# The second tile's residual sum, norm and transposes placed behind the first tile's product, at the start of a gated unit

## The chip, the cores and the metric

The kernel runs on one core of one Trainium2 chip, as one launch. The metric is device time in microseconds (us), from three timed runs of the kernel before. Beside them stands one execution that the hardware profiler recorded, and every row below comes from that one. Its engines are PE (TensorE, with PEld for its weight loads), DVE (VectorE), ACT (ScalarE), POOL (GpSimd) and SP (SyncE, whose queue issues nearly all loads).

## The reference, cut to what matters

Two blocks run one after the other over 256 tokens of width 1024. The first has two layers, and the change lies in it:

```
def swiglu(x, w_gu, w_down):
    gate, up = jnp.split(x @ w_gu, 2, axis=-1)
    return (jax.nn.silu(gate) * up) @ w_down

def hybrid_layer(x, mem_n, ...):
    h = layer_norm(DEEPNORM_ALPHA * x + 0.5 * swiglu(x, ffn1_w_gu, ffn1_w_down), ln_g[0], ln_b[0])
    ...                     # mixer: delta rule, window attention, memory attention, gates
    h = layer_norm(DEEPNORM_ALPHA * h + merged @ w_out, ln_g[1], ln_b[1])
    return layer_norm(DEEPNORM_ALPHA * h + 0.5 * swiglu(h, ffn2_w_gu, ffn2_w_down), ln_g[2], ln_b[2])
```

So each layer has two gated units (`swiglu`), and the second of them takes what the norm `ln_g[1]` gives. The second block (five mixers and a sparse expert layer that gathers table rows) is not touched.

## The kernel before, in words

**Tiles.** The 256 tokens are two tiles of 128, `x[0]` and `x[1]` (the rows name them x_74 and x_75). A gated unit multiplies with 22 column units of 1 MB each (256 columns: 128 of gate, 128 of up). A unit's weights arrive in a buffer `raw` (three of them) and are split by `unit` (line 203) into two parts of 1024 columns; of each part ACT writes a rounded copy `hi` (line 211, a CAST) and DVE, for some parts POOL, the rest `lo = raw - hi` (line 215). A product is three passes: hi by hi, hi by lo, lo by hi (`mm3`, line 232). The activations are split the same way: `transposed` (line 285) turns 128x128 pieces on PE, ACT copies four at a time to `xt0` (line 294), DVE subtracts to `xt1` (line 295).

**A gated unit (`ffn`, line 364).** The first two column units are multiplied token tile by token tile in `cols_first` (line 260; the rows call its product p_gx): 48 matmuls for the first tile, then 48 for the second. The first two units' split weights go to buffers named `hx` and, for the last `lo`, to the ring. The other 20 units (p_gu) take both tiles at once. Between them, at units 2 and 5, `mem_side` norms and transposes one tile of the memory input (`m`, with its gains `mgb`).

**The junction.** `add_norm` (line 421) loads the norm's gains and biases into `gb` (1 MB, each row of it broadcast to all partitions), and then per tile adds the residual (line 432, once per half of 512 columns), norms it (`norm`, line 297: statistics in line 304, eight one-column instructions of `rsqrt`, then lines 309 and 310 per half), and transposes it. In the kernel before it runs for both tiles in `first` (line 891) before the second gated unit of a layer begins (line 925), in the same space of buffers as the projection `out_proj`, whose last products it waits for. The gated unit at the very start has its own short form: `start(0)` loads and transposes the first tile, and `start(1)`, called by `early` behind the split of the first two units, does so for the second. Its first two units are loaded in halves of 512 KB.

**What sets the order.** The program is written through a layer with a scheduler, which fixes one order of instructions per engine when the program is built; each engine then runs its list in that order. Instructions written earlier in the program come first where the scheduler has a choice. SP's list is the order of the loads.

Of the kernel before, what the change touches and what calls it, by code (L numbers as in the profile page):

```python
# [21 lines left out]
L = 2  # L22
NT = T // P
# [4 lines left out]
ALPHA = (2 * L) ** 0.25  # L28
# [146 lines left out]
class _Kernel:  # L175
# [56 lines left out]
    def mm3(self, out, A, B, first, last):  # L232

        for n, (i, j) in enumerate(((0, 0), (0, 1), (1, 0))):
            self.nc.tensor.matmul(out, A[i], B[j], start=first and n == 0, stop=last and n == 2)  # L235
# [7 lines left out]
    def toks(self, outs, w, xt, k0, first, last):  # L243

        nk = len(w[0])
        for k in range(nk):
            for tt in range(NT):
                self.mm3(outs[tt], [t[:, tt, k0 + k] for t in xt], [t[k] for t in w],
                         first and k == 0, last and k == nk - 1)
# [7 lines left out]
                    self.mm3(outs[tt], [t[:, tt, k0] for t in xt], [t[k] for t in w], k0 == 0, k0 == n - 1)  # L257
                    k0 += 1

    def cols_first(self, name, ws, xt):  # L260

        out = []
        for tt in range(NT):
            p = self.bank([2, 2 * P], "mm", name)
            for i, w in enumerate(ws):
                for k in range(KT):
                    self.mm3(p[:, i], [t[:, tt, k] for t in xt], [t[k] for t in w], k == 0, k == KT - 1)
            out.append(p)
        return out
# [91 lines left out]
        self.nc.sync.dma_start(self.pc, self.a["pc"][l])  # L361


    def ffn(self, l, which, xt, side=(), early=None):


        nc = self.nc
        ht = [self.work.tile([P, NT, NF, P], F32R, tag=f"ht{i}", name=f"ht{i}", bufs=1) for i in range(2)]
        gu, dn = self.a["gu" + which], self.a["dn" + which]
        side = list(side)  # L370
        ws = [self.unit(gu[l, f], KT, 2 * P, LO if early else 0, None if early else self.in_work(6, ("hi", "lo")[:2 - f]), pieces=2 if early else 1)
              for f in range(2)]
        if early:
            early()
        for tt, p in enumerate(self.cols_first("p_gx", ws, xt)):
            s = self.work.tile([P, 2, P], F32, tag="silu", name="silu", bufs=2)
            h = self.work.tile([P, 2, P], F32, tag="hid", name="hid", bufs=2)
            nc.scalar.activation(s, p[:, :, :P], AF.Silu)
            nc.vector.tensor_mul(h, p[:, :, P:], s)
            self.transposed(h.rearrange("p a b -> p (a b)"), 2, ht, tt)  # L380
        for f in range(2, NF):
            w = self.unit(gu[l, f], KT, 2 * P)
            p = self.bank([2, T], "mm", "p_gu")
            for j in range(2):
                self.feat(p[:, j], w, xt, j * P)
            s = self.work.tile([P, T], F32, tag="silu", name="silu", bufs=2)
            h = self.work.tile([P, T], F32, tag="hid", name="hid", bufs=2)
            nc.scalar.activation(s, p[:, 0], AF.Silu)
            nc.vector.tensor_mul(h, p[:, 1], s)
            h = h.rearrange("p (t c) -> p t c", t=NT)  # L390
            nc.scalar.copy(ht[0][:, :, f], h)
            nc.vector.tensor_tensor(ht[1][:, :, f], h, ht[0][:, :, f].bitcast(F32), op=OP.subtract)
            if side and f % 3 == 2:
                side.pop(0)()
        y = [[self.bank([512], "acc", "p_y") for _ in range(2)] for _ in range(NT)]
        self.down(y, lambda b, **k: self.unit(dn[l, b], 2, D, **k), NF // 2, lambda b: ht, lambda b: 2 * b,
                  (self.in_work(6, ("hi",)), self.in_work(6)))
        return y
# [22 lines left out]
    def add_norm(self, l, i, x, y, coef, then=None):  # L421


        nc = self.nc
        gb = self.work.tile([P, 2, D], F32, tag="gb", name="gb", bufs=1)
        self.bcast(gb.rearrange("p a b -> p (a b)"), self.a["ln"][3 * l + i], 2 * D)
        xt = self.xt_tiles()
        for tt in range(NT):
            z = x[tt]
            for h in range(2):  # L430
                sl = slice(512 * h, 512 * h + 512)
                nc.vector.scalar_tensor_tensor(z[:, sl], y[tt][h], coef, z[:, sl], op0=OP.mult, op1=OP.add)
            self.norm(z, z, gb, LN_EPS / ALPHA ** 2)
            if then:
                then(z, xt, tt)
            else:
                self.transposed(z, KT, xt, tt)
        return xt

    def x_tile(self, tt):  # L440
        return self.state.tile([P, D], F32, tag=f"x{tt}", name=f"x{tt}", bufs=1)
# [449 lines left out]
    def first(self):  # L891
        nc, a, tc = self.nc, self.a, self.tc
        x = [self.x_tile(tt) for tt in range(NT)]
        xt = self.xt_tiles()
        self.memkv, self.memkv2 = {}, {}
        mems = [(a["mem"], "ln", a["ln"][3 * L])] * 2 + [(a["mem2"], "rms", a["nrm"][2 * L + l]) for l in range(L)]
        with tc.tile_pool(name="kv", bufs=1) as kv:
            for l in range(L):
                for k in range(2):
                    n = 2 * l + k  # L900
                    with self.space(f"f{n}"):
                        early = None
                        if n == 0:
                            def start(tt):
                                nc.sync.dma_start(x[tt], a["x"][:, tt])
                                self.transposed(x[tt], KT, xt, tt)

                            start(0)
                            early = lambda: (start(1), self.load_gain(0))
                        memT, side = self.mem_side(*mems[n])  # L910
                        y = self.ffn(l, str(k + 1), xt, side, early)
                        xt = self.add_norm(l, 2 * k, x, y, 0.5 / ALPHA, None if n < 2 * L - 1 else self.rms_xt)
                        if n < L:
                            self.memkv[n] = self.mem_kv(n, memT, kv)
                        else:
                            self.memkv2[n - L] = self.mem_kv2(n - L, memT)
                    if k == 0:
                        with self.space(f"m{l}"):
                            merged = self.work.tile([P, NT, D], F32, name="merged", bufs=1)
                            with self.space(f"mi{l}"):  # L920
                                self.load_small(l, ROW_AT["pool_scale"][0])
                                self.mixer(l, x, xt, merged)
                            with self.space(f"mo{l}"):
                                y = self.out_proj(l, merged)
                                xt = self.add_norm(l, 1, x, y, 0.5 / ALPHA)
        return x, xt


# [577 lines left out]
```

## Time and profile before

| | |
|---|---|
| median of 3 runs (lowest to highest) | 3100.79 us (3097.57 to 3101.62) |
| the profiled execution, its own time | 3095.72 us |
| its span, first to last instruction | 3093.9 us |
| mean granted TensorE clock | 0.979 |
| PE busy | 2770.6 us, 90% of the span |
| DVE busy | 2131.5 us, 69% |
| ACT busy | 1490.1 us, 48% |
| PE share of the chain that ended last | 48% |

Busy PE time comes from modelled ends of pipelined matmuls, so 90% is a share of time in which PE had something in flight. The first half of the span (the first block, to about 1420 us) is a chain of PE work, and the second half is mostly waiting for gathered table rows. The mean clock of 0.979 says that PE runs at the upper of its two levels (2.4 GHz) nearly always, and at the lower one (1.2 GHz) in short stretches.

The two junctions that the change moves lie at 500 to 530 us (layer 0) and 1215 to 1245 us (layer 1), and the program's start at 0 to 24 us.

### The profile page before, as it was taken

Reading aid. Unit: us, or ns where it says so; the run is one execution under the profiler, and the core shown is the slowest. Engines: PE = TensorE matmul, PEld = TensorE weight load, DVE = VectorE, ACT = ScalarE, POOL = GpSimd, SP = SyncE. Lnnn points to the kernel's source line nnn. Section 1 sums busy time; section 2 is a strip of 40 time slices with the busy share of each in tenths; the row PEclk is TensorE's granted clock in tenths of the full one; section 3 lists DMA queues with packets and bytes.
Section 4 is the critical chain, followed back from the end, with each engine's and each line's share of the span. In section 5 each row is a group of like instructions: output and inputs, shape, how many; then the busy total and the mean of one; then the engine's idle time right before and its main releaser. Section 6 shows DMA issues by size and latency. Waiting matters only on the chain.

```text
span 3093.9 us, 40461 instructions
## 1 busy us (share of the span) xinstructions
PE 2770.6 (90%) x13968; PEld 2000.1 (65%) x13968; DVE 2131.5 (69%) x4878; ACT 1490.1 (48%) x3196; POOL 814.4 (26%) x596
## 2 busy tenths in 40 slices
PE   9999999999999999999979887877789788978777
PEld 8988988989989887997855443322258544423222
DVE  6558667656558658657976776867578777777764
ACT  5446444444436444544645544544446454445444
POOL 0003220000003221000124444554411344445553
PEclk9999999999999999999989999999999899999999
DMA  7545325555554334556259999999962699999998
GB/s 262 182 171 176 116 89 205 197 194 194 183 184 171 116 109 149 205 186 220 82 195 425 426 421 423 427 427 427 427 229 75 264 426 426 422 426 427 426 427 347
DMA packets 121739, 841.82 MB, mean 272 GB/s; under 512 B 14016, under 2 KB 16832, under 8 KB 22208
## 3 DMA queue, kind: packets, MB, share of 16 engines
q0 software_dynamic: 73728, 536.90, 41.3%
q1 hardware_dynamic: 47520, 301.82, 27.4%
q8 instruction: 111, 1.82, 0.2%
q14 instruction: 92, 0.75, 0.1%
q10 hardware_dynamic: 288, 0.52, 0.0%
HBM read 838.15 MB, written 1.05 MB: 271 GB/s over the span
## 4 chain that ended last, share of the span: by engine, by line
PE 48%; DMA 22%; DVE 20%; issue 4%; ACT 3%; POOL 2%; POOLq 0%; DVEq 0%; SPq 0%; ACTq 0%
DMA uv<-in_puv_dram,idx 18%; PE p_gu L235 15%; PE p_y L235 11%; DVE uv L1391 5%; PE p_g L235 4%; DMA raw<-in_puv_dram,idx 4%; PE p_y L1399 2%; PE p_b L235 2%; POOL uv L1388 2%; PE p_gx L235 1%; DVE lo L215 1%; PE p_s L235 1%; DVE conv L542 1%; PE p_c L235 1%; PE p_tr L292 1%
## 5 line engine op out<-in xcount | busy, mean ns | idle before, releaser
L1399 PE MATMUL p_y<-uv,dgw 128*128 128x512 f32 x1788 | 868.6, 623 | 221.5 <-ACT dgw L1397 220.1
L1399 PEld LDWEIGHTS p_y<-uv,dgw 128*128 128x128 f32 x1788 | 324.8, 195 | 722.0 <-ACT dgw L1397 438.4
L1391 DVE SCALAR_TENSOR_TENSOR uv<-uv,xg 128x1024 f32<-128x1024 f32 x447 | 542.9, 1221 | 290.3 <-DMA uv<-in_puv_dram,idx 149.1
L211 ACT CAST hi<-raw 128x1024 fp32r<-128x1024 f32 (+1 forms) x488 | 502.3, 1034 | 472.8 <-PE p_gu L235 121.8
L215 DVE TENSOR_TENSOR lo<-raw,hi 128x1024 fp32r<-128x1024 f32 (+1 forms) x410 | 501.8, 1229 | 310.0 <-ACT hi L211 301.6
L1388 POOL DMA_INDIRECT uv<-in_puv_dram,idx x447 | 529.3, 1184 | 671.5 <-PE p_y L1399 248.4
L215 POOL TENSOR_TENSOR lo<-raw,hi 128x1024 fp32r<-128x1024 f32 (+1 forms) x78 | 197.3, 2530 | 1499.6 <-ACT hi L211 1276.8
L235 PE MATMUL p_gu<-xt,hi 128*128 128x256 f32 x2560 | 463.6, 284 | 0.0
L1394 ACT ACTIVATE wt<-act,rms_r 128x1 f32<-128x1 f32 x512 | 150.3, 294 | 569.2 <-DVE uv L1391 486.1
L235 PEld LDWEIGHTS p_gu<-xt,hi 128*128 128x128 f32 x2560 | 399.3, 192 | 0.0
L235 PE MATMUL p_gu<-xt,lo 128*128 128x256 f32 x1280 | 362.6, 283 | 0.0
L235 PEld LDWEIGHTS p_gu<-xt,lo 128*128 128x128 f32 x1280 | 245.6, 192 | 0.0
L1397 ACT ACTIVATE dgw<-ident,wt 128x128 f32<-128x128 f32 x512 | 205.0, 400 | 15.2
L235 PE MATMUL p_y<-hi,ht 128*128 128x512 f32 x576 | 181.3, 395 | 0.0
L235 PE MATMUL p_c<-xt,hi 128*128 128x256 f32 x960 | 179.8, 287 | 0.2
L1399 PE MATMUL p_y<-raw,dgw 128*128 128x512 f32 x260 | 129.8, 622 | 32.6 <-ACT dgw L1397 32.4
L1395 ACT ACTIVATE wt<-wt,gate 128x1 f32<-128x1 f32 x512 | 150.6, 294 | 16.0
L235 PEld LDWEIGHTS p_c<-xt,hi 128*128 128x128 f32 x960 | 150.6, 192 | 1.9 <-ACT sh L1095 0.7
L235 PE MATMUL p_c<-xt,lo 128*128 128x256 f32 x480 | 137.3, 287 | 0.0
L235 PE MATMUL p_y<-lo,ht 128*128 128x512 f32 x320 | 126.3, 395 | 0.0
L235 PE MATMUL p_g<-hi,xt 128*128 128x512 f32 x384 | 125.6, 400 | 0.0
L235 PEld LDWEIGHTS p_y<-hi,ht 128*128 128x128 f32 x576 | 108.5, 188 | 25.2
(524 smaller groups left out, 4275.2 us busy)
## 6 DMA issues: line engine op xcount, KB each, us to landing
raw<-in_gu_dram SPq DMA_DIRECT2D x86, 1024.0 KB, 4.8
raw<-in_dn_dram SPq DMA_DIRECT2D x44, 1024.0 KB, 4.8
raw<-in_win_t_dram SPq DMA_DIRECT2D x30, 1024.0 KB, 4.8
raw<-in_win_g_dram SPq DMA_DIRECT2D x24, 1024.0 KB, 4.8
raw<-in_wout_dram SPq DMA_DIRECT2D x18, 1024.0 KB, 4.9
raw<-in_wq_dram SPq DMA_DIRECT2D x16, 1024.0 KB, 9.4
raw<-in_wbr_dram SPq DMA_DIRECT2D x12, 1024.0 KB, 4.8
raw<-in_win_s_dram SPq DMA_DIRECT2D x8, 1024.0 KB, 6.9
```

The source lines that it names most:

```text
L211: self.nc.scalar.copy(hi, r)
L215: engine.tensor_tensor(lo[:, a:b], r[:, a:b], hi[:, a:b].bitcast(F32), op=OP.subtract)
L235: self.nc.tensor.matmul(out, A[i], B[j], start=first and n == 0, stop=last and n == 2)
L292: nc.tensor.transpose(p[:, j], x[:, (g + j) * P:(g + j + 1) * P], self.ident)
L542: nc.vector.scalar_tensor_tensor(c[:, s:], th[:, j, :T - s], pc[:, 4 * f + 3 - s:4 * f + 4 - s], c[:, s:], op0=OP.mult, op1=OP.add)
L1388: nc.gpsimd.indirect_dma_start(out=r, out_offset=None, in_=a["puv"], in_offset=bass.IndirectOffsetOnAxis(ap=idx[:, tt, h, k:k + 1], axis=0))
L1391: dot = nc.vector.scalar_tensor_tensor(r[:, :D], r[:, :D], 1.0, xg[tt], op0=OP.mult, op1=OP.mult, accum_out=act)
L1394: nc.scalar.activation(wt, act, AF.Gelu, scale=rs[tt])
L1395: nc.scalar.activation(wt, wt, AF.Copy, scale=gate[:, tt, h, k:k + 1])
L1397: nc.scalar.activation(dg, self.ident, AF.Copy, scale=wt)
L1399: nc.tensor.matmul(y[tt][half], dg, r[:, D + 512 * half:D + 512 * half + 512], start=n == 0, stop=n == HEADS * TOPK - 1)
```

## The change

`cols_first` gets a function `arrive` and calls it for each tile just before that tile's product. `add_norm` no longer runs its loop over tiles; it loads the gains and returns `arrive(tt)`, which does what the loop did for one tile. For the second gated unit of each layer this `arrive` is handed to `ffn`, where the first two units' weights are already split (in program order) when it is called for tile 0, and tile 0's product stands between it and tile 1. `add_norm` now also takes its buffers from the gated unit's space, where `gb` and `mem_side`'s `mgb` share one buffer. At the end of a gated unit both tiles are called at once, as before. At the start of the program the loads of `x[0]` and `x[1]` both stand behind the first two units.

```diff
-    def cols_first(self, name, ws, xt):
+    def cols_first(self, name, ws, xt, arrive):
...
         for tt in range(NT):
+            arrive(tt)
             p = self.bank([2, 2 * P], "mm", name)
...
-        if early:
-            early()
-        for tt, p in enumerate(self.cols_first("p_gx", ws, xt)):
+        for tt, p in enumerate(self.cols_first("p_gx", ws, xt, arrive)):
...
         xt = self.xt_tiles()
-        for tt in range(NT):
+
+        def arrive(tt):
             z = x[tt]
...
-        return xt
+
+        return xt, arrive
...
-                        early = None
                         if n == 0:
-                            def start(tt):
+                            def arrive(tt):
                                 nc.sync.dma_start(x[tt], a["x"][:, tt])
                                 self.transposed(x[tt], KT, xt, tt)
-
-                            start(0)
-                            early = lambda: (start(1), self.load_gain(0))
+                                if tt:
+                                    self.load_gain(0)
+                        elif k == 1:
+                            xt, arrive = self.add_norm(l, 1, x, y, 0.5 / ALPHA)
+                        else:
+                            arrive = lambda tt: None
                         memT, side = self.mem_side(*mems[n])
-                        y = self.ffn(l, str(k + 1), xt, side, early)
-                        xt = self.add_norm(l, 2 * k, x, y, 0.5 / ALPHA, None if n < 2 * L - 1 else self.rms_xt)
+                        y = self.ffn(l, str(k + 1), xt, side, arrive, n == 0)
+                        xt, arrive = self.add_norm(l, 2 * k, x, y, 0.5 / ALPHA, None if n < 2 * L - 1 else self.rms_xt)
+                        for tt in range(NT):
+                            arrive(tt)
...
                                 y = self.out_proj(l, merged)
-                                xt = self.add_norm(l, 1, x, y, 0.5 / ALPHA)
```

The scheduler's new order shows at three places. (Line numbers behind line 264 are one higher in the changed kernel up to `ffn`; line 309 of before is line 310 there, and 310 is 311.)

First, DVE at the junction of layer 0 in the kernel before, from the first tile's last gain (x_74) to the second tile's (x_75):

```order
L310 SCALAR_TENSOR_TENSOR x_74<-x_74,ln_r,gb 128x512 x2
L432 SCALAR_TENSOR_TENSOR x_75<-p_y,x_75 128x512
L304 BN_STATS ln_st<-x_75 128x6
L295 TENSOR_TENSOR xt_4921<-p_tr,xt_4920 128x512 x2
L305 BN_AGGR ln_mv<-ln_st 128x2
L276 TENSOR_SCALAR rs_w<-ln_mv 128x1
L309 SCALAR_TENSOR_TENSOR x_75<-x_75,ln_mv,gb 128x512 x2
```

The first tile is finished before the second tile's last residual sum (L432), and no weight split (L215) stands between them.

The same place on DVE in the changed kernel, from behind that residual sum and its statistics:

```order
L215 TENSOR_TENSOR hx<-raw,hx 128x1024
L306 BN_AGGR ln_mv<-ln_st 128x2
L215 TENSOR_TENSOR hx<-raw,hx 128x1024
L277 TENSOR_SCALAR rs_w<-ln_mv 128x1
L215 TENSOR_TENSOR lo<-raw,hx 128x1024
L278 TENSOR_SCALAR rs_y<-rs_w 128x1
L310 SCALAR_TENSOR_TENSOR x_74<-x_74,ln_mv,gb 128x512 x2
L310 SCALAR_TENSOR_TENSOR x_75<-x_75,ln_mv,gb 128x512 x2
L215 TENSOR_TENSOR lo<-raw,hx 128x1024
L215 TENSOR_TENSOR lo<-raw,hi 128x1024 x2
L279 TENSOR_TENSOR rs_h<-rs_y 128x1
L305 BN_STATS ln_st<-m 128x6 x2
```

The next row there is the first tile's last gain (L311 on x_74). Six weight splits, both tiles' L310 and the memory tile's statistics have moved ahead of it. In layer 1 the order is the same but for those statistics.

Second, PE at the same junction, before:

```order
L292 MATMUL p_tr<-ident,x_74 128x128 x8
L292 MATMUL p_tr<-ident,x_75 128x128 x8
L235 MATMUL p_gx<-hx,xt_4920 128x256 x3
L235 MATMUL p_gx<-hx,xt_4921 128x256
L235 MATMUL p_gx<-hx,xt_4920 128x256 x2
```

And in the changed kernel:

```order
L293 MATMUL p_tr<-ident,x_74 128x128 x8
L235 MATMUL p_gx<-hx,xt_4925 128x256 x2
L235 MATMUL p_gx<-hx,xt_4926 128x256
L235 MATMUL p_gx<-hx,xt_4925 128x256 x2
L235 MATMUL p_gx<-hx,xt_4926 128x256
```

The second tile's eight transposes (x_75) have left this place and stand, in two groups of four, inside the products.

Third, SP's loads at the program's start, before (x_74 is the first token tile) and changed:

```order
L355 DMA ident<-in_c_ident_dram 128x128
L905 DMA x_74<-in_x_dram 128x1024
L200 DMA raw<-in_gu_dram 128x1024 x4
L905 DMA x_75<-in_x_dram 128x1024
L331 DMA gain<-in_nrm_dram 128x1024
```

In the changed kernel the same five read:

```order
L356 DMA ident<-in_c_ident_dram 128x128
L200 DMA raw<-in_gu_dram 128x1024 x4
L905 DMA x_74<-in_x_dram 128x1024
L905 DMA x_75<-in_x_dram 128x1024
L332 DMA gain<-in_nrm_dram 128x1024
```

The first token tile's load has gone from the second place to the sixth of SP's loads. At the junctions `gb` is loaded behind three weight units where it stood behind one, and `mgb`, which now waits for the last reader of `gb`, behind six where it stood behind three.

## Rows read from the trace of the kernel before

**Rows 1.** Timeline of PE, layer 0: start, duration (us), instruction, count, idle before.
```profile
504.90 2.96 PE L235 MATMUL p_y<-hx,xt 128*128 128x512 f32 x12
507.90 1.29 PE L292 MATMUL p_tr<-ident,x 128*128 128x128 f32 x8
514.53 1.94 PE L292 MATMUL p_tr<-ident,x 128*128 128x128 f32 x8 [5.33 <-DVE x L310]
516.12 5.51 PE L235 MATMUL p_gx<-hx,xt 128*128 128x256 f32 x38
```

**Rows 2.** Chain in order of time (start, us, what, count): the product p_gx in layers 0 and 1.
```profile
516.47 12.05 PE p_gx L235 x96
...
1231.81 12.67 PE p_gx L235 x96
```

**Rows 3.** Windows of layer 0: length, PE, PEld, DVE, ACT, POOL, clock, DMA.
```profile
512.00:514.50 2.50, 0.00 (x0) 0.00 (x0) 2.33 (x10) 0.00 (x0) 0.00 (x0) 0.50 0.48 197
...
516.10:518.00 1.90, 1.90 (x12) 1.90 (x11) 1.56 (x3) 1.90 (x4) 0.00 (x0) 0.57 0.05 9
518.00:520.00 2.00, 2.00 (x19) 2.00 (x18) 2.00 (x3) 1.57 (x2) 0.00 (x0) 1.00 0.23 33
...
560.00:646.00 86.00, 86.00 (x718) 85.96 (x717) 47.74 (x61) 41.37 (x61) 0.00 (x0) 1.00 0.52 181
```

**Rows 4.** Timeline of DVE, layer 0.
```profile
507.01 1.41 DVE L310 SCALAR_TENSOR_TENSOR x<-x,ln_r,gb 128x512 f32<-128x512 f32 x2
508.34 0.68 DVE L432 SCALAR_TENSOR_TENSOR x<-p_y,x 128x512 f32<-128x512 f32 x1
509.06 0.69 DVE L304 BATCH_NORM_STATS2 ln_st<-x 128x6 f32<-128x512 f32 x1
...
512.66 0.16 DVE L278 TENSOR_TENSOR rs_h<-rs_y 128x1 f32<-128x1 f32 x1
...
513.63 1.41 DVE L310 SCALAR_TENSOR_TENSOR x<-x,ln_r,gb 128x512 f32<-128x512 f32 x2
514.96 1.22 DVE L215 TENSOR_TENSOR hx<-raw,hx 128x1024 fp32r<-128x1024 f32 x1
...
518.96 2.35 DVE L215 TENSOR_TENSOR lo<-raw,hx 128x1024 fp32r<-128x1024 f32 x2
...
523.50 1.28 DVE L304 BATCH_NORM_STATS2 ln_st<-m 128x6 f32<-128x512 f32 x2
```

**Rows 5.** Timeline of ACT, layer 0.
```profile
503.74 1.05 ACT L211 CAST hi<-raw 128x1024 fp32r<-128x1024 f32 x1 [1.80 <-PE p_y L235]
...
509.72 1.05 ACT L211 CAST hx<-raw 128x1024 fp32r<-128x1024 f32 x1
515.66 0.59 ACT L294 CAST xt<-p_tr 128x512 fp32r<-128x512 f32 x1 [4.89 <-PE p_tr L292]
516.14 1.05 ACT L211 CAST hx<-raw 128x1024 fp32r<-128x1024 f32 x1
```

**Rows 6.** DMA issues on the page: KB each, median us to landing.
```profile
raw<-in_gu_dram SPq DMA_DIRECT2D x86, 1024.0 KB, 4.8
...
raw<-in_wq_dram SPq DMA_DIRECT2D x16, 1024.0 KB, 9.4
```

**Rows 7.** Timeline of all engines, program's start.
```profile
5.05 1.94 PE L292 MATMUL p_tr<-ident,x 128*128 128x128 f32 x8 [5.05 <-DMA x<-in_x_dram]
...
6.79 0.69 DVE L295 TENSOR_TENSOR xt<-p_tr,xt 128x512 fp32r<-128x512 f32 x1 [6.79 <-ACT xt L294]
...
11.75 1.04 ACT L211 CAST hi<-raw 128x1024 fp32r<-128x1024 f32 x1 [0.19 <-DMA raw<-in_gu_dram]
```

**Rows 8.** Chain in order of time: the first product, from 12.56 us.
```profile
12.56 2.79 PE p_gx L235 x21
16.21 7.43 PE p_gx L235 x62
```

**Rows 9.** Waits of PE, 1440 to 1490 us: waiter, releaser, us, times.
```profile
PE p_cv L1063 <- DVE rs_h L278: 2.7, 1, 2.7
```

More of the change, by code (lines that the diff above doesn't have):

```diff
@@ L361, in load_small, with ffn @@
         self.nc.sync.dma_start(self.pc, self.a["pc"][l])
-    def ffn(self, l, which, xt, side=(), early=None):
+    def ffn(self, l, which, xt, side, arrive, early=False):
         nc = self.nc
```

## The prediction, before the changed kernel was run

> **What bounds the kernel now.** I read the chain of waits first: through both junctions and the start it runs over PE, so a microsecond by which a product starts later is a microsecond of the end, unless PE later waits for something else. Whether it does, the windows say: in the 86 us behind layer 0's junction PE is busy in 86.00 [rows 3]. Nothing there can take a delay back.
>
> Then I read the timeline of PE at the junction. The projection's last matmul ends at 504.90 + 2.96 = 507.86, the first tile's transposes run at once (507.90), and PE idles 5.33 us until DVE has the second tile's gains ready; its transposes start at 514.53 and the product at 516.12 [rows 1]. In layer 1 the product of 96 matmuls looks the same [rows 2]. The change aims at those 5.33 us, twice.
>
> The timeline of DVE tells what DVE must do in that gap. Here the first tile's gains (line 310) are done by 508.34, before the second tile's last sum [rows 4]. That is the row that the new order undoes.
>
> At the start the transposes wait until 5.05 for the first token tile, and the four weight pieces land one after the other, the last at 11.75 [rows 7].
>
> **The change, layer 0.** No arithmetic is added or removed; I add up DVE's new list from the end of the projection. The durations in the timeline overlap a little, so I use distances between starts: from 518.96 to 523.50 are four subtractions of 128x1024, 1.135 each; the pair of gains from 513.63 to 514.96 is 0.665 each; sum to statistics is 509.06 - 508.34 = 0.72 [rows 4].
>
> - The second tile's last sum waits for 507.86 alone, since DVE no longer runs the first tile's gains there: start 508.0.
> - Sum and statistics: 0.72 + 0.6 = 1.3, to 509.3.
> - Six weight splits: 6 x 1.135 = 6.8. Their casts are ready: ACT is past its wait for the projection at 503.74 + 1.05, and four casts of 1.05 end near 509.0 [rows 5].
> - Both tiles' first norm step, 4 x 0.665 = 2.7. `gb` is now issued behind three weight units, but had all of this time to land.
> - The memory tile's statistics, 1.24, and aggregation and three one-column steps, 0.35.
>
> The first tile's last gain so starts at 508.0 + 1.3 + 6.8 + 2.7 + 1.6 = 520.4, where it started at 507.01 [rows 4]. Its transposes start 514.53 - 513.63 = 0.9 behind it [rows 1, 4]: 521.3. PE idles 13.4 us, from 507.86, where it idled 5.33.
>
> The product needs both halves of the split activations. ACT's cast comes 515.66 - 514.53 = 1.13 behind the transposes and lasts 0.59 [rows 1, 5], so two matmuls can run by 523.3; the third needs DVE's subtraction. Before that stand the first tile's gains (1.33), nine one-column instructions at about 0.15 (1.4; one of 0.16 in [rows 4]), the second tile's gains (1.33) and one more small step: 520.4 + 4.2 = 524.6, and with 0.69 for the subtraction [rows 7] 525.3. In the kernel before the third matmul stood at 516.12 + 0.4 = 516.5 [rows 1]. That is +8.8. The second tile's eight transposes, which stood ahead of 516.12, now stand inside the product: +0.8 (the eight of the first tile take 1.29 with the last one's tail [rows 1]).
>
> The clock: in the gap it is at 0.50, and it is back at 1.00 by 518.0, with 12 matmuls in 1.90 us before and 19 in 2.00 behind [rows 3]. Before, PE ran from 514.53 with little pause until then. Now it stops again for two microseconds behind the first transposes, so somewhat more of the product runs at 1.2 GHz: +0.2, and between 0 and 1.5 (some fifteen matmuls at 0.16 instead of 0.105).
>
> What else it moves: SP's `mgb` now waits for the second tile's gains, near 524.5, and takes 4.8 us as other 1 MB loads do [rows 6], so 529.4. Behind it on DVE stands the memory tile's norm (two steps, 2.0), and queued behind that is the second tile's activation split, ready near 532.1. PE gets there after 48 matmuls and the transposes, 525.3 + 48 x 0.126 + 0.4 = 531.8 (12.05 / 96 = 0.126 [rows 2]). I count 0; the bound is the 9.4 us that loads take when the queue is full [rows 6], +4.6.
>
> Sum for layer 0: 8.8 + 0.8 + 0.2 = 9.8.
>
> One rule of the Trainium skill bears on this: the page Perfetto Trace Analysis (section Tensor Engine Instruction) says that ACT, DVE and GpSimd are strictly first in, first out. The trace agrees: ACT stood idle 4.89 us for a transpose while a cast of a half-used, long loaded weight buffer stood right behind it and ran next, at 516.14 [rows 5]. If instead DVE took what is ready, the first tile's gains would run at 508 as before, which is the third rival below.
>
> **Layer 1.** The same list without the memory tile's statistics on DVE, -1.24, and with one more small step, +0.15. The product before took 12.67 there instead of 12.05 [rows 2], low clock that the longer gap pays in both kernels, so -0.4. Sum: 8.3.
>
> **The start.** The first token tile goes behind four weight pieces of the same 512 KB. It takes the place of the fourth, which landed at 11.75 [rows 7], instead of 5.05. Its transposes then run to 11.75 + 1.94 = 13.7, and the third matmul may start 6.79 + 0.69 - 5.05 = 2.4 behind 11.75: 14.2. The weights, all cast by 12.8, no longer hold it. Before, the product was held by weights: by 12.56 it had done 96 - 21 - 62 = 13 matmuls, and 83 stood left [rows 8]. Now 94 are left at 14.2. So: 14.2 - 12.56 = 1.6, plus 11 matmuls at 0.12 (7.43 / 62) = 1.3, plus about 1.1 for the lower clock, at which eight transposes take 1.94 instead of 1.29 [rows 1, 7] and which the 13 early matmuls had used up before. Sum 4.0. It would be 0 if the load could land beside the weights, and 6.7 if all of the tile's delay counted.
>
> **The rest.** In the second block some small DVE steps change places with weight splits; one such wait is 2.7 us long [rows 9], so I take 0 and keep 1.5 either way. The second gated units' later weight splits have more time than before; PE does not wait for them now, so nothing is gained.
>
> Sum: 9.8 + 8.3 + 4.0 = 22.1. On the profiled execution's own 3095.72 that is 3117.8. The median of the runs lies 5.07 above that execution, so I predict 3100.79 + 22.1 = 3122.9, rounded 3123.
>
> **The rivals.**
>
> 1. Part is hidden. The token tile's load may land early (-4.0), and the product, with all weights split before it starts, runs without its early waits: 12.05 against 96 x 0.12 = 11.5 [rows 2, 8], -0.5 per layer. 3123 - 5 = 3118, and a little of the second block's 1.5 takes it to 3116. Against it: the pieces land in the order of issue in the trace.
> 2. `mgb` comes late. It holds DVE, and DVE holds the second tile's split. With 9.4 us instead of 4.8 it costs up to 4.6 in layer 0 and about 3 in layer 1 (half the size), plus low clock of 1.5 per layer: 3133. For it: three loads are issued just ahead of it. Against: those weights are wanted late, and each lands in 4.8 when PE is the bound.
> 3. Not slower: DVE runs the first tile's gains as early as before, at 507 to 508.3, so its split is done by 511 and the product starts there, 5.1 us earlier than 516.12, less 0.8 for the moved transposes: -4.3 per layer, -8.6, and with 4.0 at the start 3100.8 - 4.6 = 3096. It decides where line 310's gains of x_74 stand on DVE against the six weight splits: if ahead, this case; if behind, mine. In the list they stand behind.
> 4. The change does not do what it says, in that no product covers the second tile's norm. This is part of my forecast: the second tile's gains end before the first tile's product can take its third matmul, so only the transposes move behind it.
>
> **How the numbers follow.** The forecast (3119 to 3128) gets 0.70, rival 1 (down to 3112) 0.12, rival 2 (up to 3136) 0.12, rival 3 and anything else at or under 3107 0.06. A change of 0.2%, 6.2 us, is about what a measurement of this kernel can tell from none. Slower therefore 0.95, same 0.03, faster 0.02. Adding the scatter of the runs (4 us between lowest and highest) and the bounds of the clock and of `mgb`, the range is 3112 to 3132.
>
> **What would show it.** In the changed profile PE should idle about 13 us behind the projection in both layers, released by DVE's line 311 (its last gain). DVE should show four or more subtractions of 128x1024 between the second tile's statistics and the first tile's last gain. The product's bulk should begin near 525 in layer 0, counted from the same start plus 4. At the start the first transposes should wait for the token tile until about 11.8. The prediction is wrong if PE's gap is below 8 us, if the gap is as forecast but PE idles less later, or if the start costs nothing.

## The result: 0.63% slower, as forecast

| | us |
|---|---|
| kernel before, median of 5 runs (lowest to highest) | 3101.62 (3097.57 to 3104.99) |
| changed kernel, median of 5 runs | 3120.57 (3114.67 to 3123.90) |
| ratio, 95% interval | 1.0063 [1.0052, 1.0075] |
| the ratio in us | +19.5 [+16.1, +23.3] |
| predicted | 3123 (3112 to 3132), +22.1 |
| the profiled execution's own time (span) | 3114.67 (3112.9), before 3095.72 (3093.9) |

Busy times hardly moved: PE 2772.8 us (2770.6 before), DVE 2130.1 (2131.5), ACT 1490.6 (1490.1). The same work is done; what grew is waiting.

### The profile page after: what moved, and what is told of

It is laid out like the page before. It is cut to its first block, busy times and chain, and to the rows that moved or that the text cites. A ratio compares the mean times of both kernels' runs of the same rounds, so it can differ in the third digit from the quotient of the medians.

```text
span 3112.9 us, 40459 instructions
## 1 busy us (share of the span) xinstructions
PE 2772.8 (89%) x13968; PEld 2003.1 (64%) x13968; DVE 2130.1 (68%) x4878; ACT 1490.6 (48%) x3196; POOL 813.6 (26%) x596
## 5 line engine op out<-in xcount | busy, mean ns | idle before, releaser
L215 DVE TENSOR_TENSOR lo<-raw,hi 128x1024 fp32r<-128x1024 f32 (+1 forms) x410 | 500.1, 1225 | 325.3 <-ACT hi L211 309.0
L215 POOL TENSOR_TENSOR lo<-raw,hi 128x1024 fp32r<-128x1024 f32 (+1 forms) x78 | 197.4, 2532 | 1519.5 <-ACT hi L211 1519.5
```

The costliest lines, as they stand in the source:

```text
L215: engine.tensor_tensor(lo[:, a:b], r[:, a:b], hi[:, a:b].bitcast(F32), op=OP.subtract)
```

## The profile after

The timeline of PE in the changed kernel answers to [rows 1] and [rows 7]: the start, layer 0's junction, the first matmul behind that gated unit (p_mk), layer 1's junction, and the first p_cv of the second block.

```profile
11.22 1.94 PE L293 MATMUL p_tr<-ident,x 128*128 128x128 f32 x8 [11.22 <-DMA x<-in_x_dram]
...
206.81 0.41 PE L235 MATMUL p_mk<-memT,hi 128*128 128x256 f32 x2
...
509.78 2.96 PE L235 MATMUL p_y<-hx,xt 128*128 128x512 f32 x12
525.90 1.94 PE L293 MATMUL p_tr<-ident,x 128*128 128x128 f32 x8 [13.16 <-DVE x L311]
527.67 0.80 PE L235 MATMUL p_gx<-hx,xt 128*128 128x256 f32 x2
529.25 2.93 PE L235 MATMUL p_gx<-hx,xt 128*128 128x256 f32 x12 [0.79 <-DVE xt L296]
531.98 1.04 PE L293 MATMUL p_tr<-ident,x 128*128 128x128 f32 x4
532.69 1.64 PE L235 MATMUL p_gx<-hx,xt 128*128 128x256 f32 x11
...
721.59 0.41 PE L235 MATMUL p_mk<-memT,hi 128*128 128x256 f32 x2
...
1233.53 2.96 PE L235 MATMUL p_y<-hx,xt 128*128 128x512 f32 x12
1248.47 1.94 PE L293 MATMUL p_tr<-ident,x 128*128 128x128 f32 x8 [11.98 <-DVE x L311]
...
1504.74 3.71 PE L1067 MATMUL p_cv<-hp,dg 128*128 128x256 f32 x10 [2.68 <-DVE rs_h L279]
```

The same marks in the kernel before, as far as they are not in [rows 1] and [rows 7]:

```profile
202.01 0.41 PE L235 MATMUL p_mk<-memT,hi 128*128 128x256 f32 x2
...
706.90 0.41 PE L235 MATMUL p_mk<-memT,hi 128*128 128x256 f32 x2
...
1220.24 2.96 PE L235 MATMUL p_y<-hx,xt 128*128 128x512 f32 x12
...
1482.84 5.38 PE L1063 MATMUL p_cv<-hp,dg 128*128 128x256 f32 x16 [2.68 <-DVE rs_h L278]
```

Read the pair as distances, since a late start moves everything. From the projection's end (509.78 + 2.96 = 512.74; 507.86 before) to p_mk it is 208.85 us now and 199.04 before: layer 0's junction costs 9.8. From the projection's end in layer 1 (1236.49; 1223.20) to p_cv it is 268.25 against 259.64: 8.6. PE's wait ahead of the transposes is 13.16 and 11.98 us where it was 5.33 in both, and DVE's last gain releases it. When layer 0's projection ends, the changed kernel is 4.9 us late already.

The timeline of DVE at layer 0's junction shows what fills the wait; it answers to [rows 4]:

```profile
512.77 0.69 DVE L432 SCALAR_TENSOR_TENSOR x<-p_y,x 128x512 f32<-128x512 f32 x1 [2.18 <-PE p_y L235]
513.50 0.69 DVE L305 BATCH_NORM_STATS2 ln_st<-x 128x6 f32<-128x512 f32 x1
514.11 1.21 DVE L215 TENSOR_TENSOR hx<-raw,hx 128x1024 fp32r<-128x1024 f32 x1
...
515.36 1.17 DVE L215 TENSOR_TENSOR hx<-raw,hx 128x1024 fp32r<-128x1024 f32 x1
516.51 1.22 DVE L215 TENSOR_TENSOR lo<-raw,hx 128x1024 fp32r<-128x1024 f32 x1
517.70 2.73 DVE L310 SCALAR_TENSOR_TENSOR x<-x,ln_mv,gb 128x512 f32<-128x512 f32 x4
520.35 1.22 DVE L215 TENSOR_TENSOR lo<-raw,hx 128x1024 fp32r<-128x1024 f32 x1
521.49 2.35 DVE L215 TENSOR_TENSOR lo<-raw,hi 128x1024 fp32r<-128x1024 f32 x2
523.83 1.28 DVE L305 BATCH_NORM_STATS2 ln_st<-m 128x6 f32<-128x512 f32 x2
525.02 1.40 DVE L311 SCALAR_TENSOR_TENSOR x<-x,ln_r,gb 128x512 f32<-128x512 f32 x2
...
527.12 1.41 DVE L311 SCALAR_TENSOR_TENSOR x<-x,ln_r,gb 128x512 f32<-128x512 f32 x2
528.51 1.28 DVE L296 TENSOR_TENSOR xt<-p_tr,xt 128x512 fp32r<-128x512 f32 x2
533.34 1.41 DVE L310 SCALAR_TENSOR_TENSOR m<-m,ln_mv,mgb 128x512 f32<-128x512 f32 x2 [3.09 <-DMA mgb<-in_ln_dram]
```

From 512.77 to 528.5 DVE has no pause to speak of. Six weight splits, both tiles' first norm step and the memory tile's statistics stand between the second tile's sum and the first tile's last gain (525.02). The second tile's last gain (527.12) ends before the product's third matmul (529.25): no product covers the second tile's norm.

The windows of layer 0 answer to [rows 3]; the columns are length, PE, PEld, DVE, ACT, POOL, clock, DMA.

```profile
529.20:532.70 3.50, 3.45 (x17) 3.45 (x17) 1.01 (x5) 0.00 (x0) 0.00 (x0) 0.50 0.86 300
532.70:535.00 2.30, 2.30 (x21) 2.30 (x20) 1.66 (x3) 1.87 (x2) 0.00 (x0) 0.96 0.00 0
565.00:651.00 86.00, 86.00 (x720) 86.00 (x719) 50.22 (x64) 42.44 (x61) 0.00 (x0) 1.00 0.54 196
```

Seventeen instructions go through in the first 3.5 us at a granted clock of 0.50, which is 1.2 GHz, and 21 in the next 2.3 us. Behind that PE is busy in 86.00 of 86 us, as before. Nothing is given back in the gated unit.

## Experiments

The theory that the prediction left me with: the junction costs what DVE's list puts ahead of the first tile's last gain. Open was why the list stands so. Either the splits overtake because they are called earlier (call order), or the order was laid out for gains that come late. For the second speaks the timeline of SP, first of the kernel before, then of the changed one:

```profile
487.10 0.33 SPq L200 DMA_DIRECT2D raw<-in_gu_dram  x1
487.48 0.42 SPq L331 DMA_DIRECT2D gb<-in_ln_dram  x1
```

```profile
491.98 8.28 SPq L200 DMA_DIRECT2D raw<-in_gu_dram  x3
500.31 0.43 SPq L332 DMA_DIRECT2D gb<-in_ln_dram  x1
```

`gb` went from behind one weight load to behind three, 12.8 us later (about 8 of them beyond the late start). On the chip this does not hold DVE up: in the changed kernel the load lands 6.9 us behind its issue, at 507.2, and DVE then idles from 510.6 to 512.77 with the first tile's statistics and `rsqrt` done. What keeps the gains back is their place in DVE's list.

### The start alone

```diff
 (changed kernel; in first, the added lines inside the projection's space)
-    elif k == 1:
-        xt, arrive = self.add_norm(l, 1, x, y, 0.5 / ALPHA)
...
+    xt, arrive = self.add_norm(l, 1, x, y, 0.5 / ALPHA)
+    for tt in range(NT):
+        arrive(tt)
```

> The start as changed (the first tile's input loaded behind the first two units' weights, the second tile's transposes behind the first tile's product), both junctions before a second gated unit as in the kernel before. If the start's shift lasts to the end: about 4.8 us over the kernel before (the shift of the first memory-key matmul, 202.01 to 206.81 us, in the trace of the changed kernel), so near 3106.4 us or a ratio of 1.0015, with TensorE's wait before the second gated unit 5.3 us in both layers. Rival, the later stages take it up again (a transfer or a wait that was late anyway): within 1 us of the kernel before.

Measured: 3103.02 us, ratio 1.0007 [0.9998, 1.0016], so +2.2 [-0.6, +5.0]; PE's waits at the junctions 5.3 and 5.3. The interval holds both 4.8 and nothing. The traces say more when taken together. The first p_mk starts at 201.56 to 205.42 us in seven profiles with the start as before (mean 202.74) and at 206.24 to 206.81 in three with the changed start (mean 206.48): 3.7 us. The two groups do not overlap.

### The start, three times late

```diff
 (start alone; in arrive)
-    nc.sync.dma_start(x[tt], a["x"][:, tt])
+    for _ in range(1 if tt else 3):
+        nc.sync.dma_start(x[tt], a["x"][:, tt])
```

> As the run with the start alone, but the first tile's input is loaded three times over into the same buffer, one load behind the other and with some 4 MB of other loads between, so that the first transposes wait for a load that I put at 20 to 30 us instead of 11.2 us. If a late start is passed on in full: the time rises by as much as the first activation of the trace comes later than 18.2 us (the kernel before), 12 to 20 us, ratio 1.004 to 1.0065. Rival, the later stages wait for loads of their own and take up most of it: less than half of that shift in the time.

Measured: ratio 1.0065 [1.0052, 1.0079], +20.1 [+16.1, +24.5] (3118.68 us). The first wait of PE in this trace:

```profile
27.92 1.94 PE L293 MATMUL p_tr<-ident,x 128*128 128x128 f32 x8 [27.92 <-DMA x<-in_x_dram]
...
222.88 0.41 PE L235 MATMUL p_mk<-memT,hi 128*128 128x256 f32 x2
```

The first p_mk is 20.1 us behind the mean of 202.74, and the first activation, the mark of the expectation, comes at 38.36 against 18.20, 20.2 later. The whole shift reaches the end, as far as an interval of 4 us either way tells; the rival, less than half of it, falls. So I count the 3.7 us of the changed start in full, which its own timed run is too coarse to show.

### The junctions alone

```diff
 (changed kernel; in first)
...
+    start(0)
+    early = lambda: (start(1), self.load_gain(0))
+    arrive = lambda tt: None
...
 (in ffn, behind the split of the first two units)
+    if early:
+        early()
```

> The two junctions as changed, the start as in the kernel before. If the parts add up: layer 0's junction costs 9.8 us and layer 1's 8.6 us, 18.4 us together, less the 4.3 us that the changed kernel's trace shows less in layer 1's mixer and in the expert stage: between +14 and +18.4 us, 3116 to 3120 us, ratio 1.0045 to 1.0059, with TensorE idle 13.2 and 12.0 us ahead of the first tile's transposes. Rival, the 4.3 us are given back because the start was late and not by scatter: the full 18.4 us.

Measured: 3119.86 us, ratio 1.0062 [1.0049, 1.0076], +19.2 [+15.2, +23.6], waits 13.2 and 12.0. The parts as distances, layer 0 from the projection's end to p_mk and layer 1 from the projection's end to p_cv, read off each trace as above:

| kernel | layer 0 | layer 1 |
|---|---|---|
| before | 199.04 | 259.64 |
| start alone | 199.04 | 259.72 |
| changed | 208.85 | 268.25 |
| junctions alone | 209.03 | 268.32 |

The two junctions are the larger part of the change's cost, 18.4 to 18.7 us, and repeat to 0.2 us. The timed interval does not part the forecast (+14 to +18.4) from its rival (the full 18.4). What the profiled execution showed less elsewhere is of the size of the scatter: the same stretch of layer 1, p_mk to the projection's end, takes 513.4 to 517.8 us over the eleven profiles (516.30 before, 514.90 changed), and layer 0's, p_mk to the projection's end, 305.8 to 308.6. PE's waits in layer 1's stretch are the same before and changed (11.1 us in all); the granted clock is not: in the ten us that begin 300 us behind p_mk it is 0.66 before and 0.83 changed. The four profiles with the changed junctions' list lie close together (514.8 to 515.0), so this 1.4 us may belong to the change; no run shows which.

### The first tile called ahead of the weights

```diff
 (junctions alone; in ffn)
+    if not early:
+        arrive(0)
     ws = [self.unit(...) for f in range(2)]
 (in cols_first)
-    arrive(tt)
+    if tt:
+        arrive(tt)
```

> As the run with the junctions alone, but the first tile's sum, norm and transposes are called ahead of the first two units' weights, so that only the second tile's stand behind the first tile's product. Theory of the call order (the weight splits overtake the first tile's gains because they are called earlier): TensorE's wait falls from 13.2 and 12.0 us to 6 us or less, and the time to within 6 us of the kernel before. Theory of the gain's load (the gain's buffer is now taken in the gated unit's space, its load is issued about 8 us later, behind three weight loads, and the order of VectorE is laid out for a gain that comes late): the gains still stand behind four splits, the waits stay 12 to 13.5 us and the time within 3 us of the run with the junctions alone. The list of VectorE's instructions of this kernel already stands as the second theory says; the run shows whether the time does too.

Measured: 3120.20 us, ratio 1.0067 [1.0053, 1.0080]; distances 208.94 and 268.25. The DVE timeline is the changed kernel's over again; the last gain here is line 312:

```profile
516.50 2.36 DVE L215 TENSOR_TENSOR lo<-raw,hi 128x1024 fp32r<-128x1024 f32 x2
518.84 1.28 DVE L306 BATCH_NORM_STATS2 ln_st<-m 128x6 f32<-128x512 f32 x2
520.04 1.40 DVE L312 SCALAR_TENSOR_TENSOR x<-x,ln_r,gb 128x512 f32<-128x512 f32 x2
```

Though called first, the first tile's gains still stand behind all six splits. The theory of the call order falls; that of the gain's load forecast four splits ahead of the gains, and all six stand there.

### The gain loaded early

```diff
 (junctions alone; gb and mgb from a space of their own, opened ahead of the projection's)
-    gb = self.work.tile([P, 2, D], F32, tag="gb", name="gb", bufs=1)
+    gb = self.gains.tile([P, 2, D], F32, tag="gb", name="gb", bufs=1)
...
+    with self.space(f"g{l}") as self.gains:
+        with self.space(f"mo{l}"):
+            y = self.out_proj(l, merged)
+            xt, arrive = self.add_norm(l, 1, x, y, 0.5 / ALPHA)
+        with self.space(f"f{2 * l + 1}"):
...
```

> As the run with the junctions alone, calls in the changed order, but the gain's buffer lies in a space of its own that is opened ahead of the output projection, so that its load is issued where the kernel before issues it; the memory's own gain and the last norm's share that buffer, and one of the memory's transposed tiles takes the merged branches' place. Theory of the gain's load: the first tile's gains run ahead of the six splits; TensorE waits some 4 to 6 us for the first tile's transposed halves and 3 to 4 us for the second tile's gains, which now stand behind six splits of 7.1 us and the memory tile's statistics; the product ends some 3.5 us later than in the kernel before, so about +7 us for two layers: 3108 us, ratio 1.0022. Theory of the call order: nothing changes against the run with the junctions alone, 3116 to 3120 us. If the second tile's gains are covered by the first tile's product of 5.8 us as the change means it: a few us under the kernel before.

Measured: 3100.70 us over 11 runs, ratio 1.0003 [0.9994, 1.0012]; distances 200.60 and 259.74, so +1.6 and +0.1. The timelines of SP, DVE and PE at layer 0 (the projection ends at 512.80):

```profile
492.10 0.33 SPq L200 DMA_DIRECT2D raw<-in_gu_dram  x1
492.48 0.42 SPq L332 DMA_DIRECT2D gb<-in_ln_dram  x1
```

```profile
511.95 1.42 DVE L311 SCALAR_TENSOR_TENSOR x<-x,ln_r,gb 128x512 f32<-128x512 f32 x2
...
517.94 1.27 DVE L296 TENSOR_TENSOR xt<-p_tr,xt 128x512 fp32r<-128x512 f32 x2
...
521.47 2.36 DVE L215 TENSOR_TENSOR lo<-raw,hi 128x1024 fp32r<-128x1024 f32 x2
...
526.51 1.42 DVE L311 SCALAR_TENSOR_TENSOR x<-x,ln_r,gb 128x512 f32<-128x512 f32 x2
```

```profile
512.85 1.29 PE L293 MATMUL p_tr<-ident,x 128*128 128x128 f32 x8
...
515.16 0.38 PE L235 MATMUL p_gx<-hx,xt 128*128 128x256 f32 x1 [0.62 <-DVE hx L215]
518.67 5.25 PE L235 MATMUL p_gx<-hx,xt 128*128 128x256 f32 x23 [3.13 <-DVE xt L296]
...
527.41 1.29 PE L293 MATMUL p_tr<-ident,x 128*128 128x128 f32 x8 [0.75 <-DVE x L311]
```

With `gb` issued behind one weight load again, the first tile's gains (511.95) run ahead of the splits, and 17.0 of the 18.7 us of the junctions alone are gone. The cause of the loss is that the gain's buffer moved into the gated unit's space and its load with it. This run takes buffer and load back together (with `mgb`, and one of the memory's transposed tiles moved too), so which of these the scheduler goes by is argued and not shown. My own price for this run, +7 us, was too high: I had 4 to 6 us of waiting for the first tile's halves and 3 to 4 for the second tile's gains, and the trace has 0.62 + 3.13 and 0.75, 4.5 us in all. The first tile's product does run now while DVE works on the second tile's norm. That is what the change meant, and it is worth nothing here, because DVE, not PE's order, sets when the second tile's transposes can start (526.51).

### Three splits to GpSimd

DVE's list being the bound, I gave the second half of the splits of the first three units to GpSimd, idle at the junction: with the gain early, in the kernel before, and with the junctions alone.

```diff
 (in ffn, for the first two units and the third)
-    LO if early else 0
+    LO
...
-    w = self.unit(gu[l, f], KT, 2 * P)
+    w = self.unit(gu[l, f], KT, 2 * P, LO if f == 2 else 0)
```

> As the run with the gain loaded early, and in all gated units GpSimd takes the second half of the weight splits of the first three units (three subtractions of 128x1024 less on VectorE at a junction, 3 x 1.2 = 3.5 us). If VectorE's list is what TensorE waits for: the second tile's gains, at 523.9 us with the gain early, come up to 3.5 us sooner, the activation of the third unit comes 1.2 to 3.5 us sooner after the output projection's end (29.3 us with the gain early, 27.8 us in the kernel before), and the whole is 0 to 4 us under the kernel before, 3096 to 3100 us. Rival, GpSimd's subtraction (2.5 us each, rows of the kernel before) comes later than VectorE's and the product waits for it: 1 to 2 us per junction more than with the gain early, 3103 us or more.

> The kernel before with the same three splits on GpSimd, nothing of the change: what the shares are worth alone. TensorE's wait of 5.3 us ahead of the second tile's transposes holds no split and stays; the product's first 3 to 4 us, which run behind the splits, shorten by 0 to 2 us per junction: 3096 to 3100 us. Rival, GpSimd's 2.5 us come later: up to 2 us per junction slower, 3104 us.

> As the run with the junctions alone (gain loaded late), with the same three splits on GpSimd. If the gap is the sum of VectorE's list: three subtractions of 1.2 us fewer ahead of the first tile's last gain, TensorE's waits fall from 13.2 and 12.0 us to about 9.7 and 8.5 us and the time by some 7 us, to 3113 us, ratio 1.004. Rival, the gap is set by when the gain's load lands and not by the list: waits and time as in the run with the junctions alone, 13.2 and 12.0 us and 3120 us.

Measured: with the gain early 3106.17 us, ratio 1.0020 [1.0011, 1.0030]; in the kernel before 3103.35 us, 1.0011 [1.0002, 1.0021]; with the junctions alone 3117.45 us, 1.0059 [1.0045, 1.0073], PE's first waits 12.8 and 12.8 us. My first theory missed in all three; its rival's times came in the first two, not in the third. The timelines of DVE and POOL in the last say why:

```profile
512.03 3.28 DVE L215 TENSOR_TENSOR hx<-raw,hx 128x1024 fp32r<-128x1024 f32 x1
...
515.65 0.15 DVE L278 TENSOR_SCALAR rs_y<-rs_w 128x1 int32<-128x1 int32 x1
515.84 1.69 DVE L279 TENSOR_TENSOR rs_h<-rs_y 128x1 f32<-128x1 f32 x1
```

```profile
511.88 2.35 POOL L215 TENSOR_TENSOR lo<-raw,hx 128x1024 fp32r<-128x1024 f32 x1
514.17 3.33 POOL L215 TENSOR_TENSOR lo<-raw,hi 128x1024 fp32r<-128x1024 f32 x1
```

DVE's subtraction, 1.21 us when alone, begins just behind POOL's and ends 1.1 us after POOL's end (514.23). POOL's next then takes 3.33 instead of 2.35, and a one-column multiplication on DVE, 0.16 us in [rows 4], lasts until POOL is done (517.5). The step just before it, with one input tile (515.65), takes its usual 0.15 while POOL's subtraction is open. In these rows the two engines take turns where both read two tiles. Three subtractions fewer are worth 3.5 us on DVE, and these two waits alone give 2.1 + 1.5 back. The Trainium skill, page SBUF — State Buffer, section "SBUF: two separate sides", says that a DVE instruction with two SBUF inputs and a GpSimd instruction that reads SBUF take a shared pair of ports as an exclusive lock, so that the one that starts later waits for the whole of the other; these rows agree (3.28 and 1.69 us on DVE).

With the gain early the same thing hits the first tile. The timelines of DVE and POOL:

```profile
506.30 2.33 DVE L284 SCALAR_TENSOR_TENSOR ln_r<-rs_w,rs_q 128x1 f32<-128x1 f32 x1
```

```profile
506.24 2.37 POOL L215 TENSOR_TENSOR hx<-raw,hx 128x1024 fp32r<-128x1024 f32 x1 [30.30 <-ACT hx L211]
```

The last one-column step ahead of the first tile's gains waits for POOL, and PE's first transposes, which had no wait with the gain early alone, now wait 2.22 us. In the kernel before with the shares, two of DVE's subtractions take 2.09 and 3.41 us beside POOL's.

### The memory's gain not loaded

```diff
 (changed kernel; in first)
-    memT, side = self.mem_side(*mems[n])
+    memT, side = self.mem_side(*mems[n], self.gb if k else None)
```

> The changed kernel without the memory's own gain load: at each junction the memory tile's norm uses the junction's gain (that part of the result is another), so VectorE's 3.09 us wait for that load at 533.3 us is gone. My term for that wait was nothing: time within 2 us of the changed kernel, 3118 to 3122 us, ratio 1.0057 to 1.007. Rival, the wait is passed on to the product and the memory's transposes: 3 to 6 us under the changed kernel, 3115 to 3117 us.

Measured: 3121.97 us, ratio 1.0078 [1.0064, 1.0092]; distances 209.98 and 268.27. DVE no longer waits for a load, and the time does not fall: the wait cost nothing that this run shows. Layer 0 is even 1.1 us longer; in its trace a step of the memory tile's norm now stands ahead of the second tile's last gain.

None of these kernels beats the kernel before; the one with the gain early equals it.

## Why the prediction was right, point by point

- **Layer 0, +9.8 predicted, 9.8 measured.** Counted from the projection's end, the first tile's last gain was forecast 12.5 us behind (520.4 - 507.86) and came 525.02 - 512.74 = 12.3 behind; the transposes 13.4 forecast, 13.16 measured. Two smaller terms were off and cancel. The third matmul came 16.5 us behind instead of 17.4, since the small steps between the two tiles' gains took 0.8 us (525.02 to 527.12, less 1.33 for the first pair) where I had 1.4. Against it the clock cost more than the 0.2 that I took: in the rows above PE still has 0.50 at 532.7, while before it was at 1.00 from 518.0 [rows 3], so of 9.8 about 2 us are clock and moved transposes where I had 1.0. This lay inside the bound of 1.5 that I gave it. That the two errors cancel is luck.
- **Layer 1, +8.3 predicted, 8.6 measured**, with the wait 11.98 us. The memory tile's statistics, 1.24, are the difference to layer 0's wait, as worked out. The same two errors cancel here: the third matmul (1251.96) came 15.5 us behind the projection's end, which is +6.8 where the working has +7.7, and the remaining 1.8 stands against 0.6. The -0.4 for the clock had a wrong reason: in the kernel before, the gap is 5.33 us in both layers.
- **The start, +4.0 predicted**: 3.7 by the means of ten profiles, +2.2 [-0.6, +5.0] timed. The transposes wait until 11.22 (forecast 11.75); so the token tile lands behind the weights, and rival 1, which hides the start by an early landing, falls. Its other term falls too: the product has a wait of 0.79 us in layer 0 and 0.93 in layer 1.
- **`mgb`, counted 0.** It landed 4.8 us behind its issue (528.55), as counted. DVE waited 3.09 us for it (533.34), but PE has no wait from 532.7 to p_mk, and the run without that load is no faster. Rival 2 is refuted.
- **The second block, counted 0**: p_cv to its second appearance is 829.7 us in the changed kernel, against 832.7 before and 831.3 to 833.6 in the experiments; from there to the end it is 778.4 in both. No loss there.
- **The sum.** 9.8 + 8.6 + 3.7 = 22.1, as forecast, while the timed difference is 19.5 [16.1, 23.3]. The interval holds the sum. The profiled execution alone came out at 19.0: 4.9 us late at the first projection's end, 9.8 and 8.6 at the junctions, less 1.4 in layer 1's mixer and 2.9 in the second block. Both lie near the scatter of the profiles, and no run shows whether the change gives back any of it.
- **What I did not have.** I wrote that `gb` had time to land and left it there. On the chip it had (507.2), and yet the run that takes its buffer and load back puts the first tile's gains ahead of the splits again. I took that order as given, from the list itself, so the forecast stands without this cause. Rival 3, the first tile's gains ahead of the splits, is what the kernel with the gain early does; even that was not the 3096 us that I gave it, but the time of the kernel before. The term that fails there is the product's start at 511, 3.1 us behind the projection's end: DVE's split of the activations stood behind other work until 517.94, and the third matmul came 5.9 us behind (518.67 - 512.80).
- **Rival 4** holds for the changed kernel, as forecast: only the transposes of the second tile moved behind a product.

## What to carry to other kernels

Where a step moved into another space of buffers, its load moved in the queue too, and here the list laid out at build time changed with the place of buffer and load, not with the call; look first for where the operands are loaded. A gap on PE is priced well by adding up, instruction by instruction, the list of the engine that releases it, with distances between starts instead of durations: the two gaps came out 0.2 and 0.3 us shorter than forecast, while the totals, as close, owe this to errors that cancel. And a transfer of work between two engines is worth only what they can do side by side; look at a stretch in which both run it.

## What was not expected of the hardware

- DVE's and GpSimd's two-input instructions excluded each other in all three runs with shares: 1.21 us became 3.28, 2.35 became 3.33, and 0.16 became 1.69 and 2.33.
- The program's start scatters: with the same order of loads the first p_mk came at 201.56 to 205.42 us in seven profiles, more than the change of that start is worth.
